# Attention and retention heads in pairs on the two halves of TensorE's array

## The chip, the cores and the metric

The kernel runs on one core of one Trainium2 chip. The metric is the device time of one execution in microseconds (us). Three runs of the kernel before gave 1067.65, 1068.71 and 1069.38 us.

## What is computed

Two transformer blocks run one after the other on 256 tokens of 1024 features, all in float32. The part that matters here is the mixer of the first block. Its input product gives, for the latent tokens x and for 256 context tokens, the queries, keys and values of two mixers, whose outputs are joined and go through `w_out`:

```python
def gqa_block(q, k, v):                      # 8 query heads, 2 key heads, 64 wide
    s = jnp.einsum('bqkgd,btkd->bkgqt', qg, k) * ATTN_SCALE
    p = jax.nn.softmax(s, axis=-1)
    o = jnp.einsum('bkgqt,btkd->bqkgd', p, v)
...
def step(state, qkv):                        # retention, 8 heads, forward and backward
    inner = jnp.einsum('bhid,bhjd->bhij', qc, kc) * decay_mat
    o = jnp.einsum('bhij,bhjd->bhid', inner, vc) + jnp.einsum('bhid,bhde->bhie', qc, state) * q_decay
...
mix = jnp.concatenate([att, head_group_norm(ret) * silu(g)], axis=-1) @ w_out
```

The attention sees 512 keys (context and latent), four query heads to a key head. Feed-forwards, a second mixer and an attention to a memory follow; the change leaves them as they are.

## The kernel before

The tokens stand in two tiles of 128, A and B (the context's are C and D). The weights come from memory in units of 512 KB, each [128, 1024] in float32, on SP's queue. ScalarE rounds a unit to float32r (`hi`), VectorE subtracts that from the unit (`lo`), and each product is the sum of three float32r matmuls (`mm3`, line 531). The helpers record every operation, so all of VectorE's and ScalarE's instructions have line 231, TensorE's matmuls line 247 and its transposes line 252.

The order of the work is set while the program is written. Each piece (`attention("A")`, `retention()`, `projections()`, `seg1("A")`, `memory()`, ...) is a generator that yields what its next TensorE work needs; `drive` (line 484) goes on with the first of them that `Model` (line 104) holds for ready. `Model` keeps a running estimate of each engine's time. `Tensor` (line 236) enters the matmuls in it: a float32r matmul at n + 6 cycles, a float32 one at max(4 n + 10, 514). `model.slot` says when a buffer comes free: there are two score buffers (`mm`), two for transposes (`tp`) and four accumulators (`acc`, line 281). The engines then run their lists in order, and wait on semaphores where something is late.

`attention(t)` (line 1108) takes one head after the other, for each tile. Head h belongs to key head g = h // 4. Queries and keys of key head 0 stand on partitions 0 to 63 and those of key head 1 on 64 to 127, so a score matmul (64 rows, 512 keys) uses half the rows of the array:

```python
pe.matmul(out=s, lhsT=qT[t][sl, j, :], rhs=flat(kT[sl]), start=True, stop=True)
```

VectorE takes the rows' maximum, ScalarE the exponential and its sum, TensorE turns the 128x512 probabilities in four transposes, and four matmuls with the turned probabilities as weights and 64 value columns as the moving side add up the head's output, tokens on the partitions. When all eight heads are done, VectorE divides by the sums, and TensorE turns the result for the product with `w_out`, whose unit i holds rows 128 i to 128 i + 127, that is heads 2 i and 2 i + 1 (line 683).

`retention()` (line 1144) works the same way with `scores(h)` (line 1179): two score matmuls (64 rows, 256 tokens) for a head, where even heads stand on partitions 0 to 63 and odd ones on 64 to 127. `decays(h)` makes the decay factors with four exponentials on ScalarE and two operations on VectorE, and two more on VectorE weight the scores. Six matmuls of 128x64 then give a head's output for A and B. The scores of head h + 1 are issued ahead of the outputs of head h. It starts when both attentions and the gates are done.

Of the kernel before, what the change touches and what calls it, by code (L numbers as in the profile page):

```python
# [18 lines left out]
P = 128  # L19
# [32 lines left out]
# offsets in the packed rows  # L52
# [9 lines left out]
# columns of the constants  # L62
# [41 lines left out]
class Model:  # L104
    """A running estimate (us) of when engines are free and tiles are there, for the order of emission."""
# [23 lines left out]
    def tile(self, tag, bufs, ap):  # L129
        """a new tile of a tag waits for one of the tag's slots"""  # L130
        self.base[ap.name] = self.slot(tag, bufs)
        if tag in ("mm", "acc"):
            assert self.base[ap.name] < 1e9, tag
            self.live.setdefault(tag, set()).add(ap.name)
        self.slots.setdefault(tag, []).append(ap.name)
        return ap

    def slot(self, tag, bufs, more=0):
        """when a slot (and so many more) will be free"""
# [12 lines left out]
    def stream(self, t, cycles, columns):  # L152
        """the end of a matmul that begins at t; a window's clock is full after one with enough columns"""
# [42 lines left out]
class Engine:  # L196
    """an engine's instructions, emitted and entered in the model"""
# [38 lines left out]
class Tensor:  # L236
    def __init__(self, model, pe):
        self.m, self.pe = model, pe

    def matmul(self, out, lhsT, rhs, start, stop):  # L240
        n = free_size(rhs)
        rows = lhsT.shape[0] / 128.0
        if rhs.dtype == F32R:
            self.m.op("pe", n + 6, (out,), (lhsT, rhs), 0.25, n * rows)
        else:
            self.m.op("pe", max(4 * n + 10, 514), (out,), (lhsT, rhs), 0.25, 4 * n * rows)
        self.pe.matmul(out=out, lhsT=lhsT, rhs=rhs, start=start, stop=stop)  # L247

    def transpose(self, out, in_, ident):
        n = 2 * in_.shape[0]  # L250
        self.m.op("pe", n + 4, (out,), (in_,), 0.25, n)
# [4 lines left out]
def blocks_kernel(ctx: ExitStack, tc: tile.TileContext, a, out):  # L256
# [7 lines left out]
    def load(queue, out, in_):  # L264
        """a load, after those before it"""
# [21 lines left out]
    def drop(*tiles):  # L287
        """all uses of these accumulators are emitted"""
# [34 lines left out]
    # ---- constants and small vectors  # L323
# [17 lines left out]
    # ---- what comes from memory, in units of 512 KB and in the order of first use  # L341
# [4 lines left out]
    class Unit:  # L346
        """kind: split (into two float32r parts), plain (float32 as it is), or a function that consumes it"""
# [26 lines left out]
        def load(self):  # L374
            # until the first split units, their slots take the others
# [4 lines left out]
            for c0, c1, src in self.parts:  # L380
                load(nc.sync, self.raw[:, :, c0:c1], src)
            self.there = model.ready(self.raw)

        def take(self, tag, dt):
            """the slot that is free first"""
# [23 lines left out]
        def get(self):  # L409
            """a consumer is about to use the unit"""  # L410
# [10 lines left out]
    class Ffn:  # L421
        """a feed-forward's units: chunks for a tile at a time, steps for both tiles"""
# [10 lines left out]
        def product(self, t, parts):  # L433
            """with rows of the third matrix"""
# [38 lines left out]
    # ---- threads of emission: each yields what its next PE work needs (tiles, tags of which it needs a slot, or a  # L473
    # condition) and the unit that it takes
# [28 lines left out]
            # the leading tile leaves some prepared units to the others before it goes on  # L503
# [78 lines left out]
    def table(func):  # L582
        """loads a function's table ahead of its use"""
        act(out=sm(1), in_=ident[:, 0:1], func=func)

    def t_bank(src, b, m=4):
        """up to four 128-column blocks of src [tok, features], transposed, in a bank"""
# [5 lines left out]
    def split_cols(hi, lo, gname, t, b, f=None):  # L593
        """parts of t * gain of the features (from block f)"""
# [17 lines left out]
    def xj_pair(dt=F32R):  # L612
        """transposed parts of both tiles' inputs to a product"""
# [12 lines left out]
    # ================= order of the loads  # L626
# [6 lines left out]
    def mod_unit(j, kt):  # L633
        """a block of 128 rows of section j of w_mod, weighted by silu(c) and summed"""
# [32 lines left out]
    def first(z):  # L667
# [15 lines left out]
        elif z == "o":  # L683
            u = w_unit(w_out, P * i, 1, 0, D, 2)
# [13 lines left out]
    def ffn_units(parts_in, w_down, extra=""):  # L698
        """the first and the last EDGE chunks of 256 hidden features are for a tile at a time, the others for both"""
# [57 lines left out]
    # ================= start: memory keys and values, modulation of the inputs  # L757
# [16 lines left out]
    # transposes of the memory with the gains, in parts; 1/rms of its rows is applied to the products  # L774
# [6 lines left out]
    def memory():  # L781
        """values and keys with the features on the partitions; the values are turned"""
# [36 lines left out]
    def inputs():  # L819
        """1/rms and the transposes of the four input tiles"""  # L820
# [15 lines left out]
    def mod_cols(j):  # L836
        """sum over the partitions, the features on partitions, and the bias"""
# [8 lines left out]
    def mod_first():  # L846
        """the scale of the mixer's input, for both conditions at once"""
# [883 lines left out]
```

## Time and profile before

| | |
|---|---|
| median of 3 runs | 1068.71 us (1067.65 to 1069.38) |
| span of the profiled execution | 1065.1 us |
| its own time | not listed apart; the median lies 3.6 us above the span |
| TensorE busy | 1025.0 us (96%) |
| TensorE weight loads | 896.6 us (84%) |
| VectorE busy | 710.2 us (67%) |
| ScalarE busy | 515.6 us (48%) |
| GpSimd busy | 11.7 us (1%) |
| granted TensorE clock, mean | 0.997 of full speed |
| DMA | 178 GB/s on average |

The span runs from the first to the last instruction. TensorE's busy time is the time in which at least one of its matmuls was under way; matmuls overlap in their ends, so what one costs is read from the start of one to the start of the next. A float32 matmul leaves two records, a float32r one leaves one. PEld rows are the weight loads, which have records of their own.

### The profile page before, as it was taken

The numbers are of one execution on the slowest core, as the hardware profiler recorded it, in microseconds if no ns is written. First come the engines' busy times: TensorE is split into PE (matmuls) and PEld (weight loads), VectorE is DVE, ScalarE is ACT, GpSimd is POOL, SyncE is SP. The second block draws the span as 40 slices with busy tenths as digits, with TensorE's granted clock in tenths as the row PEclk, the third lists the DMA queues.
The fourth block names the chain that finished last, engine by engine and source line by source line (L and its number), as shares of the span: only waits on it lengthen the run. The fifth ranks groups of instructions, "written<-read, shape, count | busy, mean of one in ns | idle before, by whom it ended". The sixth has DMA issues, their size and how long they took to land.

```text
span 1065.1 us, 16409 instructions
## 1 busy us (share of the span) xinstructions
PE 1025.0 (96%) x6430; PEld 896.6 (84%) x6430; DVE 710.2 (67%) x1158; ACT 515.6 (48%) x838; POOL 11.7 (1%) x31
## 2 busy tenths in 40 slices
PE   4999999999899999998999999999999999999996
PEld 3488777888889999977999998799988779999995
DVE  4979766677866565568666655667977476665664
ACT  5573335464654444446444444753255365444443
POOL 4000000000000000000000000000000000000000
PEclk9999999999999999999999999999999999999998
DMA  9836765434577686664666665485245256666651
GB/s 327 276 110 196 250 198 158 149 119 120 157 228 227 180 248 187 194 201 138 200 193 181 178 183 168 155 236 156 84 151 182 60 178 191 193 190 188 187 160 39
DMA packets 196044, 189.56 MB, mean 178 GB/s; under 512 B 6272, under 2 KB 167552, under 8 KB 195968
## 3 DMA queue, kind: packets, MB, share of 16 engines
q1 hardware_dynamic: 194096, 184.11, 56.5%
q10 hardware_dynamic: 1872, 4.41, 1.4%
q8 instruction: 50, 0.82, 0.3%
q14 instruction: 26, 0.21, 0.1%
HBM read 187.45 MB, written 1.05 MB: 177 GB/s over the span
## 4 chain that ended last, share of the span: by engine, by line
PE 82%; DVE 10%; ACT 3%; DMA 2%; issue 1%; SPq 1%; ACTq 0%; DVEq 0%
PE acc L247 41%; PE mm L247 39%; PE tp L252 3%; DVE lo L231 3%; DVE k L231 3%; DVE sm L231 2%; ACT k L231 1%; DVE macc L231 1%; DMA hi<-in_w_mod_dram 1%; ACT hi L231 1%; DMA k<-in_mem_dram 1%; DVE xj L231 1%; SPq L268 1%; DMA raw<-in_w_mod_dram 0%; ACT xj L231 0%
## 5 line engine op out<-in xcount | busy, mean ns | idle before, releaser
L231 DVE TENSOR_TENSOR lo<-raw,hi 128x1024 fp32r<-128x1024 f32 x296 | 357.0, 1223 | 169.0 <-ACT hi L231 168.3
L231 ACT ACTIVATE hi<-raw 128x1024 fp32r<-128x1024 f32 x296 | 306.9, 1056 | 187.2 <-PE acc L247 71.2
L247 PE MATMUL mm<-xj,hi 128*128 128x256 f32 x1728 | 310.4, 282 | 0.0
L247 PEld LDWEIGHTS mm<-xj,hi 128*128 128x128 f32 x1728 | 268.9, 188 | 4.6
L247 PE MATMUL mm<-xj,lo 128*128 128x256 f32 x864 | 243.2, 281 | 0.0
L247 PE MATMUL acc<-hi,kh 128*128 128x512 f32 x528 | 177.3, 397 | 1.7 <-ACT kh L231 1.1
L247 PEld LDWEIGHTS mm<-xj,lo 128*128 128x128 f32 x864 | 162.6, 188 | 0.0
L247 PEld LDWEIGHTS acc<-hi,kh 128*128 128x128 f32 x528 | 99.0, 188 | 24.1 <-ACT kh L231 2.1
L247 PE MATMUL acc<-lo,kh 128*128 128x512 f32 x264 | 103.8, 393 | 0.0
L247 PE MATMUL acc<-hi,k 128*128 128x512 f32 (+1 forms) x320 | 102.9, 390 | 0.5 <-DVE k L231 0.4
L247 PE MATMUL acc<-hi,xj 128*128 128x512 f32 (+1 forms) x288 | 91.8, 389 | 0.7 <-DVE xj L231 0.7
L231 ACT ACTIVATE k<-k 128x256 f32<-128x256 f32 (+3 forms) x48 | 24.3, 506 | 113.9 <-DVE k L231 113.9
L247 PEld LDWEIGHTS acc<-hi,k 128*128 128x128 f32 x320 | 59.2, 188 | 14.9 <-issue 2.6
L247 PE MATMUL mm<-hi,xj 128*128 128x512 f32 x192 | 64.7, 402 | 5.4 <-DVE ktm L231 2.7
L247 PEld LDWEIGHTS acc<-hi,xj 128*128 128x128 f32 x288 | 53.3, 188 | 13.4 <-DVE xj L231 1.3
L247 PE MATMUL acc<-lo,k 128*128 128x512 f32 (+1 forms) x160 | 60.9, 380 | 0.0
L252 PE MATMUL tp<-keep,k 128*128 128x128 f32 (+1 forms) x292 | 45.9, 283 | 13.2 <-DMA k<-in_mem_dram 6.7
L247 PE MATMUL acc<-xj,hi 128*128 128x256 f32 x320 | 58.2, 284 | 0.0
L252 PEld LDWEIGHTS tp<-keep,k 128*128 128x128 f32 (+1 forms) x292 | 35.5, 145 | 26.7 <-issue 6.9
L247 PEld LDWEIGHTS acc<-lo,kh 128*128 128x128 f32 x264 | 49.8, 189 | 9.3 <-issue 0.2
L247 PE MATMUL acc<-lo,xj 128*128 128x512 f32 (+1 forms) x144 | 55.0, 382 | 0.0
L231 DVE TENSOR_TENSOR k<-k,k 128x256 f32<-128x256 f32 (+4 forms) x77 | 39.4, 519 | 23.0 <-ACT k L231 22.6
(160 smaller groups left out, 1208.0 us busy)
## 6 DMA issues: line engine op xcount, KB each, us to landing
raw<-in_w_in_dram SPq DMA_DIRECT2D x50, 512.0 KB, 4.6
raw<-in_ffn_down_dram SPq DMA_DIRECT2D x44, 512.0 KB, 3.7
raw<-in_w_mod_dram SPq DMA_DIRECT2D x36, 512.0 KB, 4.6
raw<-in_w_ffn_in_dram SPq DMA_DIRECT2D x36, 512.0 KB, 4.8
raw<-in_ffn_gate_dram SPq DMA_DIRECT2D x36, 512.0 KB, 4.8
raw<-in_ffn_up_dram SPq DMA_DIRECT2D x36, 512.0 KB, 4.8
raw<-in_w_ffn_out_dram SPq DMA_DIRECT2D x22, 512.0 KB, 4.5
raw<-in_w_kv_mem_dram SPq DMA_DIRECT2D x16, 512.0 KB, 5.3
```

The costliest lines, as they stand in the source:

```text
L231: return f(**kw)
L247: self.pe.matmul(out=out, lhsT=lhsT, rhs=rhs, start=start, stop=stop)
L252: self.pe.transpose(out, in_, ident)
L268: queue.dma_start(out=out, in_=in_)
```

## The change

Both mixers take heads in pairs, one on each half of the array.

- `attention(t)`: for j = 0 to 3, head j (key head 0) and head 4 + j (key head 1) go together. Their two score matmuls stand next to each other, with a score buffer each, so that a pair needs both (`"mm+"`). The outputs have the features on the partitions: the weights are 64 value columns, the turned probabilities are the moving side, and the two heads' matmuls alternate, one to output partitions 0 to 63, the other to 64 to 127.
- The factors 1 / sum are copied to 64 columns a head by GpSimd, turned by TensorE, copied by ScalarE, and multiplied into the output by VectorE. The output needs no transposes of its own any more.
- The first four units of `w_out` are loaded in two halves of 64 partitions, rows of head i and rows of head 4 + i.
- `scores(j)` in retention issues the four score matmuls of heads 2 j and 2 j + 1, alternating, and needs both score buffers; the outputs stay as they are.
- `Tensor` enters other durations in the planner: 1.047 n + 17 cycles for float32r, max(4 n + 12, 4 m + 22) for float32 with m weight columns, half of it where two halves work at once, and 220 cycles where the shape of the array's part changes.
- Comments go.

```diff
 class Tensor:
     def __init__(self, model, pe):
-        self.m, self.pe = model, pe
+        self.m, self.pe, self.tiling = model, pe, (P, P)
+    def tile(self, lhsT):
+        tiling = tuple(max(32, 1 << (n - 1).bit_length()) for n in (lhsT.shape[0], free_size(lhsT)))
+        change = 220 if tiling != self.tiling else 0
+        self.tiling = tiling
+        return change
...
         if rhs.dtype == F32R:
-            self.m.op("pe", n + 6, (out,), (lhsT, rhs), 0.25, n * rows)
+            self.m.op("pe", 1.047 * n + 17 + change, (out,), (lhsT, rhs), 0.25, n * rows)
         else:
-            self.m.op("pe", max(4 * n + 10, 514), (out,), (lhsT, rhs), 0.25, 4 * n * rows)
+            cost = max(4 * n + 12, 4 * free_size(lhsT) + 22) / ways
+            self.m.op("pe", cost + change, (out,), (lhsT, rhs), 0.25, 4 * n * rows)
...
         elif z == "o":
-            u = w_unit(w_out, P * i, 1, 0, D, 2)
+            u = w_unit(w_out, P * i, 1, 0, D, 2) if i >= 4 else Unit((1, D), [
+                (0, D, w_out[64 * h:64 * h + 64, :].unsqueeze(1), slice(64 * g, 64 * g + 64))
+                for g, h in enumerate((i, 4 + i))], 2)
...
     def attention(t):
-        att_o[t] = pacc((P, 8, 64))
+        att_o[t] = pacc((P, 4, P))
...
-        for h in range(8):
-            g, j = divmod(h, 4)
-            yield (qT[t], kT, "mm"), None
-            s = pmm()
-            sl = slice(64 * g, 64 * g + 64)
-            pe.matmul(out=s, lhsT=qT[t][sl, j, :], rhs=flat(kT[sl]), start=True, stop=True)
...
+        for j in range(4):
+            yield (qT[t], kT, "mm+"), None
+            s = [pmm() for _ in range(2)]
+            for g in range(2):
+                sl = slice(64 * g, 64 * g + 64)
+                pe.matmul(out=s[g], lhsT=qT[t][sl, j, :], rhs=flat(kT[sl]), start=True, stop=True, ways=2)
...
             for i in range(4):
-                pe.matmul(out=att_o[t][:, h, :], lhsT=pT[:, i, :], rhs=va[:, i, 64 * g:64 * g + 64],
-                          start=(i == 0), stop=(i == 3))
+                for g in range(2):
+                    sl = slice(64 * g, 64 * g + 64)
+                    pe.matmul(out=att_o[t][sl, j, :], lhsT=va[:, i, sl], rhs=pT[g][:, i, :],
+                              start=(i == 0), stop=(i == 3), ways=2)
         r = sm(8)
         dve.reciprocal(out=r, in_=att_l[t])
-        y = k2((P, 8, 64))
-        dve.tensor_tensor(out=y, in0=att_o[t], in1=bc3(r, 8, 64), op=ALU.mult)
+        rows = k2((P, 8, 64))
+        pool.tensor_copy(out=rows, in_=bc3(r, 8, 64))
+        yield (rows, "tp"), None
+        rT = k2((P, 4, P))
+        act(out=rT, in_=t_bank(flat(rows), 0), func=ACTF.Copy)
+        y = k2((P, 4, P))
+        dve.tensor_tensor(out=y, in0=att_o[t], in1=rT, op=ALU.mult)
         drop(att_o[t])
-        yield (y, "tp"), None
         attT[t] = (k2((P, 4, P), F32R), k2((P, 4, P), F32R))
-        split_plain(*attT[t], t_bank(flat(y), 0), 0)
+        split_plain(*attT[t], y, 0)
...
-        def scores(h):
-            j, g = divmod(h, 2)
-            sl = slice(64 * g, 64 * g + 64)
-            s = pmm((P, 4, P))
+        def scores(j):
+            s = [pmm((P, 4, P)) for _ in range(2)]
             for i in range(2):
-                pe.matmul(out=flat(s[:, 2 * i:2 * i + 2, :]), lhsT=krT[sl, j, i * P:(i + 1) * P], rhs=qrT[sl, j, :],
-                          start=True, stop=True)
+                for g in range(2):
+                    sl = slice(64 * g, 64 * g + 64)
+                    pe.matmul(out=flat(s[g][:, 2 * i:2 * i + 2, :]), lhsT=krT[sl, j, i * P:(i + 1) * P],
+                              rhs=qrT[sl, j, :], start=True, stop=True, ways=2)
...
-        for h in range(8):
-            if h < 7:
-                yield "mm", None
-                w[h + 1] = scores(h + 1)
+        for j in range(4):
+            if j < 3:
+                yield "mm+", None
+                w[j + 1] = scores(j + 1)
```

How the change moves instructions shows at two places on TensorE. The first is the start of the attention. `mm` are the score buffers, `acc_1231` is A's attention output and `acc_1240` B's, `k_31` the keys and `k_32` the values of all heads; `tp` rows are transposes, those of `macc` with `ones` a sum for the modulation. The kernel before:

```order
L252 MATMUL tp_1300<-keep,k_221_1176 128x128 x4
L247 MATMUL tp_1306<-macc_1058,ones 128x512
L247 MATMUL tp_1310<-macc_1058,ones 128x512
L247 MATMUL acc_1231<-k_32_218,k_251_1283 128x64 x4
L247 MATMUL mm_1318<-k_31_217,k_204_1087 128x512
L247 MATMUL acc_1240<-k_32_218,k_253_1290 128x64 x4
L247 MATMUL mm_1329<-k_31_217,k_215_1137 128x512
```

A head's four outputs of 128x64 and one score matmul alternate between the tiles. The kernel after, at the same place:

```order
L263 MATMUL tp_1278<-keep,k_239_1237 128x128 x4
L263 MATMUL tp_1285<-keep,k_240_1238 128x128 x4
L258 MATMUL mm_1291<-k_31_217,k_216_1140 128x512
L258 MATMUL mm_1292<-k_31_217,k_216_1140 128x512
L258 MATMUL acc_1231<-k_249_1277,k_32_218 64x128
L258 MATMUL acc_1231<-k_251_1284,k_32_218 64x128
...
L258 MATMUL tp_1312<-macc_1058,ones 128x512
L258 MATMUL tp_1316<-macc_1058,ones 128x512
L258 MATMUL mm_1320<-k_31_217,k_204_1087 128x512
L258 MATMUL mm_1321<-k_31_217,k_204_1087 128x512
```

Both heads of a pair are turned one after the other, the other tile's two score matmuls stand together, and eight outputs of 64x128 follow, alternating between the heads (two are shown); between B's pair and A's next stand these eight and the two sums.

The second place is retention. `acc_2083` and `acc_2084` (after: `acc_2113` and `acc_2114`) are the outputs of A and B. The kernel before:

```order
L247 MATMUL mm_2144<-xj_396_1882,k_186_973 128x256 x2
L247 MATMUL acc_2083<-k_389_1863,xj_395_1881 128x64
L247 MATMUL acc_2083<-k_295_1479,k_448_2112 128x64
L247 MATMUL acc_2083<-k_317_1569,k_448_2112 128x64
L247 MATMUL acc_2084<-k_389_1863,xj_395_1881 128x64
L247 MATMUL acc_2084<-k_295_1479,k_448_2112 128x64
L247 MATMUL acc_2084<-k_317_1569,k_448_2112 128x64
L247 MATMUL mm_2165<-xj_396_1882,k_186_973 128x256 x2
```

Two score matmuls of one head, then six outputs of the head ahead of it. The kernel after, from the third pair on:

```order
L258 MATMUL mm_2271<-xj_402_1920,k_186_973 128x256
L258 MATMUL mm_2272<-xj_402_1920,k_186_973 128x256
L258 MATMUL mm_2271<-xj_402_1920,k_186_973 128x256
L258 MATMUL mm_2272<-xj_402_1920,k_186_973 128x256
L258 MATMUL acc_2113<-k_399_1915,xj_401_1919 128x64
L258 MATMUL acc_2113<-k_307_1541,k_457_2195 128x64
L258 MATMUL acc_2113<-k_346_1684,k_457_2195 128x64
L258 MATMUL acc_2114<-k_399_1915,xj_401_1919 128x64
L258 MATMUL acc_2114<-k_307_1541,k_457_2195 128x64
L258 MATMUL acc_2114<-k_346_1684,k_457_2195 128x64
```

Four score matmuls of two heads alternate between the halves, and twelve outputs (six are shown) stand between one pair's scores and the next's.

## Rows read from the trace of the kernel before

**Rows 1.** The page's head.
```profile
span 1065.1 us, 16409 instructions
```
**Rows 2.** Busy time by stage: us, PE, PEld, DVE, ACT, POOL, clock, DMA share, GB/s.
```profile
118.00:243.00 125.00, 125.00 (x712) 98.66 (x712) 82.72 (x138) 58.73 (x119) 0.00 (x0) 1.00 0.50 162
243.00:300.00 57.00, 53.03 (x321) 46.31 (x321) 47.92 (x101) 35.41 (x58) 0.00 (x0) 1.00 0.51 150
```
**Rows 3.** TensorE in order of time, attention scores: start, us, engine, instruction, records.
```profile
118.11 1.98 PE L247 MATMUL mm<-k,k 64*128 64x512 f32 x4
120.02 0.50 PE L247 MATMUL acc<-hi,xj 128*128 128x512 f32 x1
...
155.57 1.12 PE L247 MATMUL mm<-k,k 64*128 64x512 f32 x2
156.62 0.50 PE L247 MATMUL acc<-hi,k 128*128 128x512 f32 x1
...
163.60 1.13 PE L247 MATMUL mm<-k,k 64*128 64x512 f32 x4
164.66 0.50 PE L247 MATMUL acc<-hi,k 128*128 128x512 f32 x1
```
**Rows 4.** TensorE in order of time, retention.
```profile
218.20 1.14 PE L247 MATMUL mm<-xj,k 64*128 64x256 f32 x8
...
224.94 1.13 PE L247 MATMUL mm<-xj,k 64*128 64x256 f32 x4
225.99 0.43 PE L247 MATMUL acc<-k,xj 128*128 128x64 f32 x2
...
227.48 1.13 PE L247 MATMUL mm<-xj,k 64*128 64x256 f32 x4
```
**Rows 5.** TensorE in order of time, attention outputs and their weight loads.
```profile
161.55 1.99 PEld L247 LDWEIGHTS acc<-k,k 128*128 128x128 f32 x16
161.78 1.90 PE L247 MATMUL acc<-k,k 128*128 128x64 f32 x16
...
191.54 4.58 PE L247 MATMUL acc<-k,k 128*128 128x64 f32 x40
196.05 1.12 PE L247 MATMUL mm<-k,k 64*128 64x512 f32 x2
```
**Rows 6.** TensorE in order of time, weights of two columns.
```profile
40.60 1.88 PE L247 MATMUL acc<-hi,csil 128*2 128x512 f32 x4
42.32 1.88 PE L247 MATMUL acc<-lo,csil 128*2 128x512 f32 x4
```
**Rows 7.** TensorE in order of time, a product and a weight load.
```profile
156.96 0.40 PE L247 MATMUL acc<-lo,k 128*128 128x512 f32 x1
156.96 0.42 PEld L247 LDWEIGHTS acc<-hi,k 128*128 128x128 f32 x2
```
**Rows 8.** GpSimd's groups: shapes, count, busy us, mean ns, idle us before them.
```profile
L231 POOL TENSOR_TENSOR rope<-keep,small 128x64 f32<-128x64 f32 x4 | 1.3, 326 | 0.0
```
**Rows 9.** DMA issues: count, KB each, median us to landing.
```profile
raw<-in_w_ffn_in_dram SPq DMA_DIRECT2D x16, 256.0 KB, 4.0
```
**Rows 10.** Groups of VectorE and ScalarE, 118 to 200 us: the softmax.
```profile
L231 DVE TENSOR_REDUCE sm<-mm 128x1 f32<-128x512 f32 x15 | 10.3, 687 | 5.1 <-PE mm L247 5.0
L231 DVE TENSOR_SCALAR sm<-sm 128x1 f32<-128x1 f32 x15 | 2.3, 153 | 0.5
...
L231 ACT ACTIVATE k<-mm,sm 128x512 f32<-128x512 f32 x15 | 10.3, 690 | 33.9 <-DVE sm L231 33.7
L231 ACT ACTIVATION_READ_ACCUMULATOR k<-mm,sm 128x1 f32 x15 | 2.9, 193 | 0.0
```
**Rows 11.** Groups of VectorE and ScalarE, 218 to 243 us: the decays.
```profile
L231 DVE TENSOR_TENSOR k<-mm,k 128x256 f32<-128x256 f32 x16 | 6.0, 419 | 2.9 <-PE mm L247 2.4
L231 DVE TENSOR_TENSOR k<-k,keep 128x128 f32<-128x128 f32 x8 | 2.3, 291 | 0.3
...
L231 ACT ACTIVATE k<-k,lg 128x128 f32<-128x128 f32 x32 | 10.4, 392 | 5.6 <-DVE k L231 5.6
```

More of the change, by code (lines that the diff above doesn't have):

```diff
@@ L237, in __init__, with matmul @@
     def __init__(self, model, pe):
-        self.m, self.pe = model, pe
-    def matmul(self, out, lhsT, rhs, start, stop):
+        self.m, self.pe, self.tiling = model, pe, (P, P)
[4 more added lines that the diff above has]
+        return change
+    def matmul(self, out, lhsT, rhs, start, stop, ways=1):
         n = free_size(rhs)
         rows = lhsT.shape[0] / 128.0
+        change = self.tile(lhsT)
         if rhs.dtype == F32R:
-            self.m.op("pe", n + 6, (out,), (lhsT, rhs), 0.25, n * rows)
+            self.m.op("pe", 1.047 * n + 17 + change, (out,), (lhsT, rhs), 0.25, n * rows)
         else:
-            self.m.op("pe", max(4 * n + 10, 514), (out,), (lhsT, rhs), 0.25, 4 * n * rows)
+            cost = max(4 * n + 12, 4 * free_size(lhsT) + 22) / ways
+            self.m.op("pe", cost + change, (out,), (lhsT, rhs), 0.25, 4 * n * rows)
         self.pe.matmul(out=out, lhsT=lhsT, rhs=rhs, start=start, stop=stop)
@@ L250, in transpose @@
         n = 2 * in_.shape[0]
-        self.m.op("pe", n + 4, (out,), (in_,), 0.25, n)
+        self.m.op("pe", n + 6 + self.tile(in_), (out,), (in_,), 0.25, n)
         self.pe.transpose(out, in_, ident)
@@ L379, in load @@
             self.raw = raw.rearrange("p (a b) -> p a b", a=self.shape[0])
-            for c0, c1, src in self.parts:
-                load(nc.sync, self.raw[:, :, c0:c1], src)
+            for c0, c1, src, *rows in self.parts:
+                load(nc.sync, self.raw[rows[0] if rows else slice(0, P), :, c0:c1], src)
             self.there = model.ready(self.raw)
@@ L1131, in attention @@
             for i in range(4):
-                pe.matmul(out=att_o[t][:, h, :], lhsT=pT[:, i, :], rhs=va[:, i, 64 * g:64 * g + 64],
-                          start=(i == 0), stop=(i == 3))
+                for g in range(2):
+                    sl = slice(64 * g, 64 * g + 64)
+                    pe.matmul(out=att_o[t][sl, j, :], lhsT=va[:, i, sl], rhs=pT[g][:, i, :],
+                              start=(i == 0), stop=(i == 3), ways=2)
         r = sm(8)
         dve.reciprocal(out=r, in_=att_l[t])
-        y = k2((P, 8, 64))
@@ L1177, in decays @@
             return e1, off
-        def scores(h):
-            j, g = divmod(h, 2)
-            sl = slice(64 * g, 64 * g + 64)
-            s = pmm((P, 4, P))
+        def scores(j):
+            s = [pmm((P, 4, P)) for _ in range(2)]
             for i in range(2):
-                pe.matmul(out=flat(s[:, 2 * i:2 * i + 2, :]), lhsT=krT[sl, j, i * P:(i + 1) * P], rhs=qrT[sl, j, :],
-                          start=True, stop=True)
-            e, off = decays(h)
-            w = k2((P, 4, P))
-            dve.tensor_tensor(out=w[:, 0:4:3, :], in0=s[:, 0:4:3, :],
-                              in1=e.unsqueeze(1).to_broadcast([P, 2, P]), op=ALU.mult)
-            dve.tensor_tensor(out=w[:, 1:3, :], in0=s[:, 1:3, :], in1=off, op=ALU.mult)
-            drop(s)
+                for g in range(2):
+                    sl = slice(64 * g, 64 * g + 64)
+                    pe.matmul(out=flat(s[g][:, 2 * i:2 * i + 2, :]), lhsT=krT[sl, j, i * P:(i + 1) * P],
+                              rhs=qrT[sl, j, :], start=True, stop=True, ways=2)
+            w = []
+            for g in range(2):
+                e, off = decays(2 * j + g)
+                w.append(k2((P, 4, P)))
+                dve.tensor_tensor(out=w[g][:, 0:4:3, :], in0=s[g][:, 0:4:3, :],
+                                  in1=e.unsqueeze(1).to_broadcast([P, 2, P]), op=ALU.mult)
+                dve.tensor_tensor(out=w[g][:, 1:3, :], in0=s[g][:, 1:3, :], in1=off, op=ALU.mult)
+                drop(s[g])
@@ L1192, in scores @@
             return w
-        yield (qrT, krT, "mm"), None
+        yield (qrT, krT, "mm+"), None
         w = {0: scores(0)}
-        for h in range(8):
-            if h < 7:
-                yield "mm", None
-                w[h + 1] = scores(h + 1)
-            wh = w.pop(h)
-            yield (wh, qfT["A"], qfT["B"]), None
-            for i, t in enumerate("AB"):
-                o = ret_o[t][:, h, :]
-                pe.matmul(out=o, lhsT=qfT[t][:, h, :], rhs=state[:, h, :], start=True, stop=False)
-                for k, u in enumerate("AB"):
-                    pe.matmul(out=o, lhsT=wh[:, 2 * k + i, :], rhs=vr[u][:, h, :], start=False, stop=(k == 1))
+        for j in range(4):
+            if j < 3:
+                yield "mm+", None
+                w[j + 1] = scores(j + 1)
+            for g, wh in enumerate(w.pop(j)):
+                h = 2 * j + g
+                yield (wh, qfT["A"], qfT["B"]), None
+                for i, t in enumerate("AB"):
+                    o = ret_o[t][:, h, :]
+                    pe.matmul(out=o, lhsT=qfT[t][:, h, :], rhs=state[:, h, :], start=True, stop=False)
+                    for k, u in enumerate("AB"):
+                        pe.matmul(out=o, lhsT=wh[:, 2 * k + i, :], rhs=vr[u][:, h, :], start=False, stop=(k == 1))
```

23 lines of the change are left out of this document (12 added, 11 removed).

## The prediction

> **What bounds the kernel now.** I read the page's head first, then a table of stages, then TensorE's instructions in order of time through the stage that the change touches, and last what VectorE and ScalarE spend there. The span is 1065.1 us [rows 1]. [...] The next stage, 243 to 300 us, already holds 4.0 us of TensorE idle time [rows 2].
>
> Does a pair of matmuls on the two halves of the array run at once? The kernel before answers this for the row halves by accident. It issues a score matmul (64 rows, 512 columns) for one head at a time, and each leaves two records. One alone holds TensorE for 1.05 us, from 155.57 to the next product at 156.62. Two that follow each other on the *same* row half (head 0 of tile A and head 0 of tile B) take 1.91 us, 118.11 to 120.02. Two that follow each other on *different* halves (head 5 of A, head 3 of B) take 1.06 us, 163.60 to 164.66 [rows 3]. The same shows in retention: heads 0 and 1 together, eight records, are busy for 1.14 us; a head alone, four records, for 1.13 [rows 4]. So the second matmul of a pair on row halves is free.
>
> **The change part by part.**
>
> *Attention scores.* Before: two same-half couples (118.11 and one more like it) at 1.91, one lucky couple at 1.06 and ten single ones at 1.05, together 15.4 us. After: eight pairs at 1.06, 8.5 us. Saved: 6.9 us.
>
> *Retention scores.* Before: one couple at 1.07 and six single heads at 1.05 (224.94 to 225.99) [rows 4], 7.4 us. After: four pairs at 1.07, 4.3 us. Saved: 3.1 us.
>
> *Attention outputs.* Before: 64 matmuls of 128x64. Twenty of this shape (the state's 16 and a head's 4) take 191.54 to 196.05, so 0.2255 us each [rows 5]; the 64 take 14.4 us. They are bound by their weights of 128 columns: eight matmuls from 161.78 have 1.90 us of matmul and 1.99 us of weight loads [rows 5]. After: still 64, but the weights are 64 value columns, and the 128 probabilities stream past. Their stream, by the couple of score matmuls on one half, is (1.91 - 0.20) / 2 = 0.855 us for 512 columns, so 0.214 for 128. The 0.20 us is what a half-array group has over its stream (1.05 - 0.855) when the matmuls around it use the whole array; the eight output groups become such groups and pay it too. The trace has no two matmuls on different *column* halves: two with weights of 2 columns, in the same column place, follow each other at 1.72 / 2 = 0.86 us, without overlap [rows 6]. So the price of an output group lies between 4 x 0.214 + 0.20 = 1.06 us (halves at once) and 8 x 0.214 + 0.20 = 1.91 us (one after the other): eight groups take 8.5 or 15.3 us, which saves 5.9 us or loses 0.9. I take the first, since the nearest rows are those of the row halves, where a pair costs what one costs; even if the two halves' loads take turns, half of 0.2255 twice is no more than the stream.
>
> [...] In the trace the weight load that begins at 156.96 runs beside the product that begins at 156.96 [rows 7], and both use all rows of the array. [...]
>
> *The rest.* The four transposes of each tile's output become four of its factors, at the same price: nothing. GpSimd copies the factors to 512 elements, twice; a 64-element operation took 0.33 us there [rows 8], so at most eight times that, 2.6 us, and ScalarE copies once more. The factors need the exponentials' sums alone, so this runs beside the last output group, and TensorE's list has a dozen products or more from a tile's last exponential to these transposes. If they were late, TensorE would wait once a tile, 1 us or so; I count nothing. The four output-product units of 512 KB are now loaded as eight DMAs of 256 KB on SP's queue; other loads of 256 KB landed in 4.0 us [rows 9], and they are prefetched: nothing, or 1 us if a unit were late. The new durations of the planner move products, memory units and transposes by a few places up to the first feed-forward and hardly at all behind it: no work is added; I count nothing, with 2 us either way for waits that move.
>
> *What is given back.* A pair now needs both score buffers at once, and they come free when the second exponential is done. VectorE needs 2 x (0.687 + 0.153) us for a pair, and the last exponential and its sum 0.690 + 0.193 [rows 10]: 1.06 + 1.68 + 0.88 = 3.6 us from one pair's start to the next's. The new list puts 2.9 us of work between the first two such pairs (an output group and two 512-column matmuls) and about 3.3 at two other places, elsewhere far more: about 1.2 us of waits. In retention a pair costs ScalarE 8 x 0.392 = 3.1 us and VectorE 2 x (2 x 0.291 + 2 x 0.419) = 2.8 us [rows 11], beside TensorE's 1.07 + 2 x 1.49 = 4.0 (225.99 to 227.48 is one head's output) [rows 4]: close, so 0.8 us of waits. Given back: 2.0 us; between 0, and 6 if every one of the twelve pairs waits 0.5 us for an instruction ahead of it on VectorE.
>
> *Sum.* 6.9 + 3.1 + 5.9 = 15.9 us saved, 2.0 given back: 13.9. The span becomes 1065.1 - 13.9 = 1051.2. The profiled execution's time is not listed beside its span; the median of the runs, 1068.7, lies 3.6 us above the span, which I keep: **1054.8 us**.
>
> **The rivals.**
>
> *The column halves take turns.* Output groups at 1.91 us: 6.8 us less is saved, **1061.6 us**. For it: no row shows two column halves at work. Against it: the row halves overlap fully, weight loads included.
>
> *The chains behind the pairs set the pace in part.* All of a pair's softmax or decay work now falls between two steps of TensorE, and VectorE's share of the stage rises from 82.72 / 125 to 82.72 / 111. With the 6 us above and 2 us of moved waits, **1060.8 us**. Against it: the list keeps products and memory units between most pairs.
>
> *No weight load beside the other column half.* Half a load (0.113 us) before every half matmul (0.214), 64 times, and eight times 0.20: 22.5 us in place of 14.4, so the outputs lose 8.1 and the scores' 10.0 is all but spent: 1068.7 - 10.0 + 8.1 + 2.0 = **1068.8 us**, no change. [...]
>
> *Slower: both score buffers are held, and nothing covers it.* If products do not stand ready, each attention pair leaves TensorE idle for 3.6 - 1.06 = 2.5 us and each retention pair for about as much: with 2.0 us at each of twelve places, 24 us against 15.9, **1076.8 us**. It decides from 1.3 us a pair. For it: only two buffers, also used by the memory units. Against it: TensorE's list has other work between nearly all pairs, and now no wait at all is seen in this stage.
>
> **How the numbers follow.** The forecast has 0.72, column halves in turn 0.11, chains in part 0.10, no change 0.04, slower 0.03. The forecast's own range goes from 1050.5 (nothing given back, 2 us of waits fewer) to 1058.8 (6 us given back). To leave out no more than 2 in 10 the range takes in the two rivals above it, to 1062.0, and a little more below for waits that vanish elsewhere: 1050.0 to 1062.0. About 0.2% (2 us) is what a measurement of this kernel can tell from no change. Faster 0.93, same 0.04, slower 0.03.
>
> **What would show it.** In the profile after, score pairs should hold TensorE for 1.06 us each with four records in attention and 1.07 with eight in retention; an output group of sixteen records for 1.06 us (1.9 would mean halves in turn, 2.8 a load before each); the stage from the first scores to the last retention output should be some 14 us shorter, with about 2 us of TensorE idle in it, put down to VectorE or ScalarE; behind it the idle time of the next stage should stay near 4.0 us. The forecast is wrong if idle time inside the stage exceeds 6 us, or if a clock below 1.00 is granted in it.

## The result and the profile after

The kernel after took **1075.34 us** (median of 4 runs, 1075.05 to 1077.22) where the kernel before took 1068.18 beside it: 1.007 of before, 95% interval 1.0054 to 1.0086. The forecast was 1054.8. It is slower, and it is 20.5 us from the forecast. Beside each of the later groups of runs the kernel before was timed again; its medians lie between 1068.2 and 1069.0 us, so differences between kernels of two groups hold to about 1 us.

The page's head of the kernel after, with TensorE's busy time and the granted clock in 40 slices of the span:

```profile
span 1073.5 us, 16433 instructions
...
PE 1022.3 (95%) x6430; PEld 893.9 (83%) x6430; DVE 710.0 (66%) x1158; ACT 518.0 (48%) x840; POOL 12.9 (1%) x33
...
PEclk9999999978999999999999999999999999999999
```

TensorE's busy time fell by only 2.7 us (1025.0 before), and in two of the slices, from 215 to 268 us, the clock is at 0.7 and 0.8 of full speed. The time in which TensorE is idle, the span less its busy time, rose from 40.1 to 51.2 us. So there is less work, some of it done at the lower clock, and more waiting. The stages of the kernel after, in the columns of [rows 2], with the second mixer (700 to 790 us) besides:

```profile
118.00:243.00 125.00, 122.15 (x763) 98.15 (x762) 84.89 (x142) 62.14 (x123) 1.23 (x2) 0.95 0.55 170
243.00:300.00 57.00, 50.62 (x262) 41.94 (x262) 43.75 (x95) 31.73 (x53) 0.00 (x0) 0.87 0.44 131
700.00:790.00 90.00, 84.94 (x677) 81.45 (x676) 65.92 (x102) 33.98 (x39) 0.00 (x0) 1.00 0.50 150
```

and the second mixer of the kernel before:

```profile
700.00:790.00 90.00, 89.33 (x698) 86.03 (x697) 70.02 (x116) 35.05 (x40) 0.00 (x0) 1.00 0.50 152
```

Idle TensorE time went from 0 to 2.85 us in the stage of the change, from 4.0 to 6.4 in the next, and from 0.7 to 5.1 in the second mixer, which the change does not touch.

**The pairs do what was forecast.** TensorE in order of time in the kernel after (start, us, instruction, records), an attention pair, its outputs, and the first retention pair:

```profile
124.27 1.13 PE L258 MATMUL mm<-k,k 64*128 64x512 f32 x4
125.33 1.09 PE L258 MATMUL acc<-k,k 128*64 128x128 f32 x16
126.35 1.13 PE L258 MATMUL tp<-macc,ones 128*128 128x512 f32 x2
...
210.04 1.14 PE L258 MATMUL mm<-xj,k 64*128 64x256 f32 x8
```

From 124.27 to 125.33 a pair of score matmuls holds TensorE for 1.06 us, which is what the couple on different halves took in [rows 3]. The output group, eight matmuls of 128 columns and four of them on each half, takes 1.02 us, from 125.33 to 126.35: the column halves work at once. Its sixteen weight-load records, from 125.32 on, take 0.85 us in all. The first retention scores begin at 210.04 us, 8.2 us earlier than in [rows 4].

**Then the clock falls.** The same view, retention from the third pair on; in brackets the idle time ahead of an instruction and what ended it (`<-DVE k`: VectorE, writing a tile `k`):

```profile
224.58 1.14 PE L258 MATMUL mm<-xj,k 64*128 64x256 f32 x8
225.64 0.43 PE L258 MATMUL acc<-k,xj 128*128 128x64 f32 x2
225.91 0.61 PE L258 MATMUL acc<-k,k 128*128 128x64 f32 x4
226.36 0.39 PE L258 MATMUL acc<-k,xj 128*128 128x64 f32 x2
...
229.15 0.67 PE L258 MATMUL mm<-xj,k 64*128 64x256 f32 x2 [0.61 <-DVE k L231]
230.53 2.04 PE L258 MATMUL mm<-xj,k 64*128 64x256 f32 x6 [0.72 <-DVE k L231]
232.51 0.69 PE L258 MATMUL acc<-k,xj 128*128 128x64 f32 x2
232.99 1.06 PE L258 MATMUL acc<-k,k 128*128 128x64 f32 x4
233.84 0.63 PE L258 MATMUL acc<-k,xj 128*128 128x64 f32 x2
...
243.53 0.77 PE L258 MATMUL acc<-hi,k 128*128 128x512 f32 x1 [0.53 <-DVE k L231]
...
247.11 0.77 PE L258 MATMUL acc<-hi,k 128*128 128x512 f32 x1 [1.95 <-DVE k L231]
```

Two outputs (four records) take 0.45 us at 225.91 and 0.85 us at 232.99: 0.22 against 0.43 each, at a granted clock of 1.00 and of 0.50 of full speed. The clock's own record has 0.50 from 230.2 us for 20.5 us. Ahead of the fall stand a score pair, the narrow outputs of two heads (64 columns each) and two waits for VectorE, which has to read a score buffer before the fourth pair may overwrite it. The kernel before had 1.00 in all of this stage [rows 2].

### The profile page after: what moved, and what is told of

Read it like the earlier page. It is cut to its first block, busy times and chain, and to the rows that moved or that the text cites. A ratio compares the mean times of both kernels' runs of the same rounds, so it can differ in the third digit from the quotient of the medians.

```text
span 1073.5 us, 16433 instructions
## 1 busy us (share of the span) xinstructions
PE 1022.3 (95%) x6430; PEld 893.9 (83%) x6430; DVE 710.0 (66%) x1158; ACT 518.0 (48%) x840; POOL 12.9 (1%) x33
## 5 line engine op out<-in xcount | busy, mean ns | idle before, releaser
L263 PE MATMUL tp<-keep,k 128*128 128x128 f32 (+1 forms) x292 | 45.6, 285 | 17.7 <-DVE k L231 8.5
```

What stands on the lines that cost most here:

```text
L263: self.pe.transpose(out, in_, ident)
```

## The experiments

### Which part costs: pairs and durations taken apart

Four kernels, put together from the two at hand.

Before, with the change's new durations alone (those of the transposes, n + 6 for n + 4, are among them):

```diff
+            self.m.op("pe", 1.047 * n + 17 + change, (out,), (lhsT, rhs), 0.25, n * rows)
...
+            cost = max(4 * n + 12, 4 * free_size(lhsT) + 22) / ways
```

> The kernel before with only the planner's new durations; no heads in pairs. Theory C (pairing retention lets TensorE's clock fall, and the new durations cost some 7 us in waits behind it): clock 1.00 through retention, about 1075 us, with idle time at the second block's mixer as in the kernel after. Rival D (the new durations alone place the work badly, and the clock falls from that): granted clock near 0.5 for some 20 us in retention, 1078 us or more. If durations cost nothing: 1068 us.

Both pairings, with the durations of before (`ways` without effect):

```diff
-            self.m.op("pe", 1.047 * n + 17 + change, (out,), (lhsT, rhs), 0.25, n * rows)
+            self.m.op("pe", n + 6, (out,), (lhsT, rhs), 0.25, n * rows)
...
-            cost = max(4 * n + 12, 4 * free_size(lhsT) + 22) / ways
+            self.m.op("pe", max(4 * n + 10, 514), (out,), (lhsT, rhs), 0.25, 4 * n * rows)
```

> The kernel after with the planner's old durations. Theory C: attention saves about 11 us, retention still loses its clock for some 20 us and gives about 10 us back, the late waits of the new durations are gone: about 1068 us. Rival D: clock stays at 1.00, about 1056 us.

The change with retention one head at a time:

```diff
-        def scores(j):
+        def scores(h):
...
-        for j in range(4):
+        for h in range(8):
```

> The kernel after with retention one head after the other, as before; pairs in attention and new durations stay. Theory C: clock 1.00 through retention, 1068 - 11 + 7 = 1064 us. Rival D: the clock falls here too, 1073 us or more.

Before, with the new durations and retention in pairs:

```diff
-        def scores(h):
+        def scores(j):
```

> The kernel before with pairs in retention only, and the new durations. [...] Rival D: as with the durations alone less 3 us, about 1072 us.

A fifth followed, attention in pairs with the durations of before and retention one head at a time (the second and the third edit together):

> The change's paired attention alone: the planner's durations as before, retention one head at a time as before. With both pairings and the old durations the kernel took 1065.8 us, 0.998 of before. Theory that paired retention costs time only by the waits and the clock that follow it, whatever the durations: retention one head at a time then does better than both pairings, 1060 to 1064 us. Rival, that paired retention costs only where the new durations placed it: leaving it out gives up its 3.1 us, 1067 to 1070 us.

Measured, in us, with the ratio to before and its 95% interval:

| | durations of before | new durations |
|---|---|---|
| no pairs | 1068.8 (before) | 1087.0, 1.018 (1.016 to 1.020) |
| attention in pairs | 1069.9, 1.001 (1.000 to 1.002) | 1069.8, 1.001 (1.000 to 1.003) |
| retention in pairs | not run | 1083.4, 1.015 (1.012 to 1.017) |
| both | 1065.8, 0.998 (0.997 to 0.999) | 1075.3, 1.007 (1.005 to 1.009) |

The new durations alone, which add no work, cost 18 us: theory C had 7, and rival D's slow stretch in retention is not there (a clock of 0.50 for 3.4 us only, from 265.5 us). Of the other three, C comes near in time with both pairings (1068) and with retention in pairs alone (with a slow clock in retention again, 1068 - 3 + 10 + 7 = 1082), but its slow stretch in retention is not there (0.50 for 3.4 and 6.8 us); with attention alone neither comes near. With both pairings the new durations cost 9.5 us. With them, pairs in attention save 17 us and pairs in retention 3.6 on their own, but retention's cost 5.5 on top of attention's.

The lower left of the table has the other half of the miss. With no new duration at all, both pairings gain 3.0 us and not 13.9. In that kernel's profile TensorE's busy time fell by 11.1 us (1025.0 to 1013.9), and its idle time rose by 9.9 (40.1 to 50.0, in a span of 1063.9): the work was saved, and the new order turned most of it into waiting.

One of the waits in the kernel with the durations alone, TensorE in order of time (both pairings with the durations of before have one like it, of 3.68 us):

```profile
264.62 0.39 PE L258 MATMUL mm<-k,lo 128*128 128x256 f32 x1 [3.62 <-DVE lo L231]
```

### Which of the new durations

The product's number alone, on both pairings with the durations of before:

```diff
-            self.m.op("pe", n + 6, (out,), (lhsT, rhs), 0.25, n * rows)
+            self.m.op("pe", 1.047 * n + 17, (out,), (lhsT, rhs), 0.25, n * rows)
```

> Both pairings with the old durations (1065.8 us), and of the new durations only that of the products' float32r matmuls, 1.047 n + 17 clocks in place of n + 6. Theory that this one number, 8 per cent more for each of some 3,500 product matmuls, is what shifts the order for the worse: 1072 to 1080 us, with waits for VectorE in the second mixer (700 to 790 us). Rival, that the loss comes from the other new numbers (the paired and the narrow float32 matmuls, and 220 clocks at each change of the piece's size): 1064 to 1068 us, no such waits.

**1076.8 us**, 1.0077 (1.0063 to 1.0092): 11 us for this one number. And the other way round, the change with only the product's number put back:

```diff
-            self.m.op("pe", 1.047 * n + 17 + change, (out,), (lhsT, rhs), 0.25, n * rows)
+            self.m.op("pe", n + 6, (out,), (lhsT, rhs), 0.25, n * rows)
```

> The changed kernel with only the products' duration put back to n + 6 clocks; the new numbers for paired and narrow float32 matmuls and for a change of the piece's size stay. Theory that the products' duration alone is the cause: 1062 to 1068 us, as both pairings took with all old durations (1065.8). Rival, that the other new numbers cost too: 1069 to 1075 us.

**1067.6 us**, 0.9993 (0.9984 to 1.0001): 7.8 us less than the change. So the product's duration is what costs among the new numbers. The others make 1.8 us more with the product's old number (1065.8 to 1067.6) and 1.4 less with its new one (1076.8 to 1075.3), hardly more than the 1 us to which these differences hold. One of the places at which the product's duration costs is the first feed-forward's end. TensorE in order of time in the kernel after, and then in this one:

```profile
482.41 1.75 PE L263 MATMUL tp<-keep,x_A 128*128 128x128 f32 x8 [3.74 <-DVE x_A L231]
```

```profile
478.37 1.29 PE L263 MATMUL tp<-keep,x_A 128*128 128x128 f32 x8 [0.87 <-DVE x_A L231]
```

The transposes of x_A wait 3.74 us for VectorE in the one and 0.87 in the other; which piece was moved ahead of them was not looked into.

### Is the new number wrong, or are the others too small?

The new number is the better one. Products of 512 columns in the kernel after:

```profile
122.84 0.39 PE L258 MATMUL acc<-lo,xj 128*128 128x512 f32 x1
123.07 0.39 PE L258 MATMUL acc<-hi,xj 128*128 128x512 f32 x1
```

One begins 0.23 us after the one before it; five of them, from 122.15 to 123.30, take 1.15 us. At the 2400 cycles a us of the planner's faster rate (line 158 of the kernel), 1.047 n + 17 is 553 cycles, 0.230 us, and n + 6 is 518, 0.216 us. A theory then is that the planner's VectorE and ScalarE durations are too short (it has 0.60 us for the maximum of 512 columns, [rows 10] has 0.687), and that a planner which held TensorE for too fast had covered for it. On the change:

```diff
-                cost = 0.069 + 0.06 * small + n / (1920.0 if fast and sources < 2 else 960.0)
+                cost = 0.155 + 0.06 * small + n / (1920.0 if fast and sources < 2 else 960.0)
...
-                cost = 0.08 + 0.09 * min(small, 1) + n / 1200.0
+                cost = 0.17 + 0.09 * min(small, 1) + 0.2 * ("accum_out" in aps) + n / 1200.0
```

> The changed kernel, and the planner's VectorE and ScalarE durations measured too, as its TensorE durations are: 0.155 us in place of 0.069 ahead of a VectorE operation, 0.17 in place of 0.08 ahead of a ScalarE one, and 0.2 more where it also sums. Theory that the loss comes from TensorE durations that were lengthened while those of the engines that it waits for stayed too short: the waits for VectorE's k in retention and in the second mixer go, and the kernel takes 1058 to 1066 us. Rival, that longer TensorE durations by themselves put the products' pieces in worse places: no waits are won, 1070 to 1080 us.

**1081.5 us**, 1.0123 (1.0104 to 1.0141): worse by 6. The same edit with both pairings and the TensorE durations of before:

> Both pairings with the old TensorE durations and the measured VectorE and ScalarE durations of the run with the longer ones on top of the change (which took 1081.5 us). Theory that those longer durations are good and were only spoiled by the products' new duration: 1058 to 1065 us. Rival, that they hurt by themselves (conversions of weights are put off when the two engines look busy, and TensorE then waits for them): 1070 to 1082 us.

**1088.1 us**, 1.018 (1.0167 to 1.0193): worse by 22. And, on the same, a product shorter than it was:

```diff
-            self.m.op("pe", n + 6, (out,), (lhsT, rhs), 0.25, n * rows)
+            self.m.op("pe", 0.95 * n + 6, (out,), (lhsT, rhs), 0.25, n * rows)
```

> Both pairings with the old durations, and the products' shorter still, 0.95 n + 6 clocks. Theory that a duration below the measured one leaves the planner slack, which hides its too short VectorE and ScalarE durations, and more is better: 1058 to 1065 us. Rival, that the order is tuned to no side and any shift moves some piece the wrong way or the right way by chance: anything from 1062 to 1080 us, and above 1068 decides for it.

**1085.8 us**, 1.0155 (1.0141 to 1.017): worse by 20. The theory of slack falls. A product's duration moved up or down, or the other engines' moved to what they measure, each makes the kernel slower. The four tries don't show why n + 6 is the good number; they show that the order is good for it and for no neighbour tried.

### One moved piece

In the second mixer the cause can be seen whole. In the kernel before, the recurrence's first eight score matmuls stand behind 216 products in an unbroken row, in the kernel after behind 204 (and so in the ones above with the product's new duration and the other engines' of before). The expectation below counts them otherwise, 147 and 135; the difference is twelve in both counts. TensorE in order of time, before:

```profile
724.71 1.95 PE L247 MATMUL mm<-k,k 128*128 128x128 f32 x16
729.61 2.02 PE L247 MATMUL mm<-k,k 128*128 128x128 f32 x16
```

and after:

```profile
726.33 0.61 PE L258 MATMUL mm<-k,k 128*128 128x128 f32 x4
727.70 1.60 PE L258 MATMUL mm<-k,k 128*128 128x128 f32 x12 [0.76 <-DVE k L231]
735.46 2.02 PE L258 MATMUL mm<-k,k 128*128 128x128 f32 x16 [1.89 <-DVE k L231]
```

Twelve products of 256 columns are 1.4 us of work. Without them in front, the scores arrive before VectorE's k, and TensorE, which runs its list in order, stands still for 0.76 us with independent products behind the scores; the next link of the chain waits 1.89 us more. To put back this piece and nothing else, the change with

```diff
         fT, kbT, qaT = st["hgrn"]
+        for b in model.there[qaT.name]:
+            model.there[qaT.name][b] += 1.5
```

which moves these eight matmuls behind the twelve products and leaves every other instruction of TensorE, VectorE and ScalarE where it is.

> The changed kernel with one piece put back where it stood before the change: the first eight score matmuls of the second mixer's recurrence stand behind 147 of the mixer's products again and not behind 135; nothing else is moved on TensorE, VectorE or ScalarE. Theory that a product's new duration costs time by moving single pieces to where their data comes a moment late: the waits for VectorE's k at 727.7 and 735.5 us, 2.7 us together, and the small ones behind them go, 1070 to 1073 us. Rival, that the wait only moves to the next piece of the same chain, since VectorE's and ScalarE's work in front of it is what is late: 1075 to 1076 us.

**1072.3 us**, 1.0036 (1.0022 to 1.0051): 3.1 us less than the change, and no wait at these two places:

```profile
731.55 1.95 PE L258 MATMUL mm<-k,k 128*128 128x128 f32 x16
736.45 2.02 PE L258 MATMUL mm<-k,k 128*128 128x128 f32 x16
```

(The profiled execution of this kernel has a span of 1074.7 us, above its median time, with a clock of 0.50 for 23.9 us in retention; of it only this place is read here.)

### What the slow clock costs

First the change, in its own order, with TensorE work added that the planner does not know of, before each pair's retention scores:

```diff
             s = [pmm((P, 4, P)) for _ in range(2)]
+            for g in range(2):
+                pe.pe.matmul(out=flat(s[g]), lhsT=qfT["A"][:, 0, :], rhs=flat(state), start=True, stop=True)
```

> The changed kernel in the same order, and ahead of each pair's retention scores two more float32 matmuls of 128 rows and 512 columns into the two score buffers, which the scores then overwrite: 8 in all, 0.87 us each by the trace, 7.0 us of TensorE work that the planner does not know of. [...] Rival, that the waits themselves are the cost and the clock only accompanies them: 1078 to 1083 us.

**1076.3 us**, 1.0079 (1.0064 to 1.0093). The theory was that the stretch at a clock of 0.50 costs about 10 us and goes or shrinks to under 7, and that some 3 us of the added work lie in what were waits: 1066 to 1072 us. The time lies between this range and the rival's: 7.0 us of work added and 1.0 us more time. The stretch at 0.50 shrank from 20.5 us to 6.8 (at 245.5 us). With less added, one such matmul ahead of each pair's scores, and on the kernel with the product's old duration (1067.6 us), which has the same stretch of 20.5 us from 230.0:

```diff
             s = [pmm((P, 4, P)) for _ in range(2)]
+            for g in range(1 if True else 0):
+                pe.pe.matmul(out=flat(s[g]), lhsT=qfT["A"][:, 0, :], rhs=flat(state), start=True, stop=True)
```

> [...] Rival, that the chain of VectorE's work behind retention sets the time and TensorE's clock in it costs nothing: 1069 to 1071 us.

**1064.1 us**, 0.9955 (0.9941 to 0.9969), as the theory had it: by the author's estimate the stretch costs some 6 us, since its 17.7 us of work would take half as long at a clock of 1.00 and 2.5 us of waits grow by some of that, and with the stretch gone or under 7 us the kernel takes 1062 to 1066 us. And ahead of the third and the fourth pair alone:

```diff
+            for g in range(1 if j >= 2 else 0):
```

> As the run before, with the added matmul only ahead of the third and the fourth pair's scores, 1.7 us of it, 1.3 us of which can lie in the two waits of 0.61 and 0.72 us that stand ahead of the fourth pair. Theory that these two waits are what the clock falls behind: the stretch goes or shrinks, 1060 to 1064 us. Rival, that the narrow output matmuls (64 columns each) are enough for it to fall: the stretch stays, 1067.5 to 1069.5 us.

**1062.6 us**, 0.9946 (0.9931 to 0.9961). Last, on the same kernel, retention one head at a time, without added work:

> The changed kernel with the products' old duration and retention one head at a time. Theory that paired retention saves its 3.1 us on TensorE and loses more than that by the slow stretch: without it no stretch over 7 us, 1063 to 1066 us. Rival, that retention in pairs gains about 4 us as it did with all old durations (1069.9 against 1065.8): 1070 to 1072 us.

**1063.3 us**, 0.9946 (0.9930 to 0.9962). The stretch 230 to 250.5 us in these kernels, busy times in the columns of [rows 2], the clock third from the end. The product's old duration alone:

```profile
230.00:250.50 20.50, 17.74 (x68) 15.39 (x68) 10.98 (x28) 3.68 (x5) 0.00 (x0) 0.50 0.00 0
```

with the added work ahead of the third and the fourth pair:

```profile
230.00:250.50 20.50, 16.46 (x89) 13.56 (x89) 15.33 (x33) 6.59 (x8) 0.00 (x0) 0.83 0.15 47
```

with retention one head at a time:

```profile
230.00:250.50 20.50, 18.26 (x108) 16.32 (x108) 15.89 (x30) 7.97 (x10) 0.00 (x0) 0.92 0.33 99
```

In the first TensorE is busy for 17.74 of 20.50 us, all at a clock of 0.50, and gets through 68 records; in the second it is busy for less and gets through 89. In the list of the second, the added matmul fills what were the two waits, and the waits for VectorE behind retention remain:

```profile
227.41 1.08 PE L1208 MATMUL mm<-k,xj 128*128 128x512 f32 x2
...
236.44 0.47 PE L258 MATMUL acc<-hi,k 128*128 128x512 f32 x1 [1.13 <-DVE k L231]
...
240.01 0.77 PE L258 MATMUL acc<-hi,k 128*128 128x512 f32 x1 [2.63 <-DVE k L231]
```

So 1.7 us of useless work (two matmuls at 0.86 us, [rows 6]) makes the kernel 5.0 us faster: with the two waits covered, the clock of 0.50 came only at 238.1 us and for 6.8 us. Where the 5.0 us come from can be read off the first and the last of the 24 outputs behind the fourth pair. With the product's old duration alone:

```profile
229.99 0.69 PE L258 MATMUL acc<-k,xj 128*128 128x64 f32 x2
...
239.43 1.06 PE L258 MATMUL acc<-k,k 128*128 128x64 f32 x4
```

and with the added work:

```profile
229.74 0.43 PE L258 MATMUL acc<-k,xj 128*128 128x64 f32 x2
...
234.70 0.61 PE L258 MATMUL acc<-k,k 128*128 128x64 f32 x4
```

The last line holds two outputs, so the 24 take some 10.3 us in the one and 5.4 in the other: 4.9 of the 5.0 us are these matmuls at the clock of 0.50.

Does the clock fall behind the waits, or are the narrow outputs enough? The kernel with both pairings and the durations of before has nothing added, and in its list no wait stands ahead of the fourth pair (eight transposes come behind the third pair's scores there, and ahead of them in the change):

```profile
227.95 1.14 PE L247 MATMUL mm<-xj,k 64*128 64x256 f32 x8
229.02 0.44 PE L247 MATMUL acc<-k,xj 128*128 128x64 f32 x2
...
233.98 0.61 PE L247 MATMUL acc<-k,k 128*128 128x64 f32 x4
```

The same 24 outputs take 5.4 us, and the granted clock is 1.00 up to 249.9 us. So the narrow outputs alone do not bring the fall. Among all the kernels here a stretch of 20 us or more stands in those four whose list has two waits ahead of the fourth pair (0.61 us, then 0.40 to 0.72), and in no other. How two such short waits do it is not shown.

Retention one head at a time has no such waits and reaches the same time. Its order differs at other places too, so it is no test of the clock alone.

These last two are the fastest versions found: 0.995 of before, and 12 to 13 us less than the change.

## Why the prediction was wrong

**What bounds it.** Right as far as it went: work taken off TensorE did leave its busy time (11.1 us with the durations of before). That all of it leaves the run too was the author's estimate, and no run shows it: with these 11.1 us less work the kernel took 3.0 us less. The forecast took a full TensorE in one stage (125.00 of 125.00 us, [rows 2]) as a reason to count only work; what was lost is waiting and clock.

**Scores and outputs** (6.9, 3.1 and 5.9 us). Right. A score pair holds TensorE for 1.06 us and an output group for 1.02 (1.06 forecast); a retention pair takes 1.06 us, from 224.58 to 225.64 (1.07 forecast). So the rivals *column halves in turn* (1.91) and *no weight load beside the other half* (2.8) are out. No run shows the load of 0.113 us before every half matmul that the second of them is added up from: the sixteen load records of an output group, all of 128 rows, take 0.85 us in all inside its 1.02, and the forecast's 1.06 counts no time for them.

**Given back** (2.0 us). The sum was near, 2.6 us of waits in 118 to 243 us, but by luck: no score pair of the attention waits, where 1.2 us were forecast; retention's pairs wait 1.3 us on VectorE's k (0.8 forecast), and the rest stands at places that were not thought of, VectorE's xj (0.8) and ScalarE's k (0.5). The consequence of retention's waits was not priced. The text named a clock below 1.00 in this stage as a sign that the forecast is wrong, but gave it no time; on the kernel with the product's old duration, covering two waits of 1.3 us together won 5.0 us, although it added 1.7 us of work.

**The step that failed** is the one on the planner: "no work is added; I count nothing, with 2 us either way for waits that move". The product's duration alone costs 7.8 us in the change, 3.1 of it by eight matmuls moved past twelve products, nearly 500 us behind the part that the change is about. The text said that behind the first feed-forward hardly anything moves, and took a small move for a small price. Nor is a new number needed for a new order: the pairs alone, with every duration of before, raise TensorE's idle time by 9.9 us. The other new numbers cut both ways: attention in pairs alone takes 1069.9 us with all durations of before and 1063.3 with only the product's of before, both pairings 1065.8 and 1067.6.

**The balance.** From 1075.3 us the product's duration takes 7.8 (1067.6) and the cover for the clock 5.0 (1062.6). Of the 7.8 us that are left to the forecast, up to 1.7 are the added matmuls themselves and 3.8 the waits of 1.13 and 2.63 us for VectorE behind retention, which the sum did not have. The rest, 2.3 us, was not taken apart; the clock's record of that kernel has 0.50 in four stretches, 17.1 us together, where that of the kernel before has 1.00 up to 1059.6 us of its 1065.1, and what they cost was not measured.

**The rivals.** *Both score buffers are held* gave nearly the measured time, 1076.8, and is still not what happened: it wanted 24 us of waits at the pairs, and there are 1.3 (2.6 in the whole stage). *Chains in part* has the waits behind VectorE right in kind, for 3.8 us, a fifth of the miss.

**Two slips in the working**, neither of which matters. The lower end of the forecast's own range, 2.0 us of waits not given back and 2 us fewer, is 1050.8 and not 1050.5; and half of 0.2255 us twice is slightly more, not less, than the stream of 0.214.

## What to carry to other kernels

A planner's duration is part of the order, not a note on the side: a new number, even a truer one, can be a new order, so it is priced by a run of its own, apart from the change that it comes with. And where work is taken out of a planned list, the order changes with it, so the time saved is read from the idle time as well as from the work. In an order where data arrives just in time, look in the new list for the pieces of a dependent chain that moved ahead of independent work, however few, since everything behind them in the engine's list is held up with them: here TensorE stood still for 0.76 and 1.89 us ahead of independent products. And where the granted clock falls behind short waits amid narrow matmuls, filling just these waits is worth a try, even with useless work: here two added matmuls won 5.0 us, four won 3.5, and eight, on the change, won nothing.

## What was not expected of the hardware

In the kernel with the product's old duration the clock stayed at 0.50 of full speed for 20.5 us in which TensorE was busy for 17.74 us. It did so behind two waits of 0.61 and 0.72 us, with no wait above 1.95 us within, and each output matmul went from 0.22 to 0.43 us; over 24 of them that cost 4.9 us, several times the two waits. With both pairings and the durations of before, whose list has no wait there, the same 24 outputs took 5.4 us at a clock of 1.00. And two column halves of the array, loads included (0.85 us in all), ran side by side as two row halves do (1.06 us for a score pair): four matmuls of 128 columns on each in 1.02 us.
